# An encoder layer on one core: the merge gates go to the end of the first stage, and an input is exchanged by halves

## The chip, the cores and the metric

The kernel runs on one core of a Trainium2 chip. Its time is the device time of one execution in microseconds, and the figure compared is the median of several runs. The engines are TensorE (PE, with PEld for its weight loads), VectorE (DVE), ScalarE (ACT), GpSimd (POOL) and SyncE (SP). SyncE only issues DMA transfers; all of this kernel's transfers go through its one queue, in order.

## The reference

The layer takes 2048 tokens of 1024 channels in float32. One RMS-normalised input `h` feeds three token mixers, whose outputs are merged by gates that are computed from the same `h`:

```
h = rmsnorm(x, g_mix); z = h @ w_in          # 5648 columns, 3072 of them for the gates
gates = sigmoid(gate_pre)                    # 3 branches x 1024 channels
y = gates0*(h_m @ w_proj_mlstm) + gates1*(h_na @ w_proj_na) + gates2*(h_mem @ w_proj_mem)
x = x + y @ w_out
out = x + square(relu(rmsnorm(x, g_ffn) @ w_up)) @ w_down
```

`h_m` is a bidirectional mLSTM (a recurrence over the tokens in both directions), gated by `o`, another 512 columns of `z`. `h_na` is a neighbourhood attention over a 32 x 64 grid of tokens. `h_mem` is a cross attention into 256 memory tokens.

## The kernel before

Every large product is made of three TensorE matmuls (`mm3`, L228): both factors are split into a high and a low part, and high*high, high*low and low*high are summed in PSUM. A unit of weights is a tile of 128 x 1024 values; `fetch` (L155) loads one with a DMA (`wr`) and has ScalarE and VectorE, for every fourth unit GpSimd, split it (`ws`). `take` hands units out in the order that `plan` (L139) wrote down. TensorE's instructions run in the order in which the program writes them. The order on the other engines, SyncE's queue too, is set when the program is built, by a scheduler that goes by priorities and by its own estimate of when operands are ready.

The tokens are worked on in four blocks of 512. The tile `hT` holds the split, normalised input of one block, transposed, as 8 k tiles of 128 channels; there is one such tile.

Stage 1 (`phase_1`, `block_a`) runs block by block the products with `w_in`: q and k of the attention, q and k of the mLSTM, v, gates (for blocks 2 and 3 alone, `GATES_1`), and o. Gates are 24 groups of 24 matmuls with one weight unit each (`gate`, L596); o is four groups of 24. Each group's result is taken out of PSUM by ScalarE into a tile `ev` (two buffers in stages 1 and 2) and stored. After every second k tile, `tick` (L106) lets side work go one step: the attention's small matmuls and softmax rows (`na_stream`), the cross attention, preparation of the next block's input. Blocks 0 and 1 store their `hT` to DRAM (`SPILL`).

Stage 2 (`phase_2`) runs the mLSTM's recurrence as side work (`ml_stream`, which starts after 20 ticks) beside the gates of blocks 1 and then 0, which need those inputs back (`late_gates`, L603). Gates that are left when the recurrence ends run at the start of stage 3. `ml_consts` and `ml_logsig` set up stage 2: constants, and two `ev` tiles, for the raw row of `g_mlstm` (scaled into `gml` at L710) and for the log of the forget gates. Stage 3 is the merge, the output projection and the MLP.

So `hT` is exchanged twice. The first exchange is at the end of stage 1: each o group of block 3 frees one slice of 128 tokens, and block 1's slice is loaded there (L559 to L567), the last one in eight small transfers. The second is in stage 2, between the gates of block 1 and those of block 0: four transfers of 1 MB, one for every two k tiles, and four ticks without gates (L607 to L611).

`sums_down` (L569) is other work that lies beside the gates. It prepares operands for the last product of stage 3: per call two loads of 512 KB, four VectorE subtractions (L580) and two stores of 512 KB, with low priority. It is called after every third gate, 8 times in block 2 and 8 times in block 3.

Of the kernel before, what the change touches and what calls it, by code (L numbers as in the profile page):

```python
# [12 lines left out]
F32 = mybir.dt.float32  # L13
F32R = mybir.dt.float32r
BF16 = mybir.dt.bfloat16
AF = mybir.ActivationFunctionType
# [8 lines left out]
LOW, LATER, LATER_A, SOON = 100, 60, 60, 40  # L25
TICKS_2, START_2 = 4, 20
PAD = 192
# [9 lines left out]
NB = S // TB  # L37
# [5 lines left out]
GATES_1, GATES_2 = [2, 3], [1, 0]  # L43
# [36 lines left out]
class Body:  # L80
# [58 lines left out]
    def plan(self):  # L139

        u = unit_index()
        self.down = u["down"]
        out = list(u["w_mem_kv"])
        for b in range(NB):
            for n in ("naqk", "qk", "navm", "v"):
                out += u[n]
            if b in GATES_1:
                out += u["gate"]
            out += u["o"]
        for g in GATES_2:  # L150
# [341 lines left out]
    def block_a(self, b):  # L492
# [42 lines left out]
        for t in range(4):  # L535
# [5 lines left out]
            self.store(self.scr["v"][b][t * 128:(t + 1) * 128], s)  # L541
        if b in GATES_1:
            for j in range(24):
                if j == 22 and b + 1 < NB:
                    self.prep_x()
                self.gate(b, j)
                if j % 3 == 2:
                    self.sums_down(8 * GATES_1.index(b) + j // 3)
        w = self.take(4)
        for t in range(4):  # L550
# [7 lines left out]
            self.store(self.scr["og"][b][t * 128:(t + 1) * 128], s)  # L558
            if b == NB - 1:  # L559
                ts = slice(t * 128, (t + 1) * 128)  # L560
                src = self.scr["hT"][GATES_2[0]]
                if t < 3:
                    nc.sync.dma_start(hT[:, :, :, ts].bitcast(F32), src[:, :, :, ts])
                else:
                    for k in range(0, 8, 2):
                        for l in range(2):
                            nc.sync.dma_start(hT[:, l, k:k + 2, ts].bitcast(F32), src[:, l, k:k + 2, ts])  # L567

# [27 lines left out]
    def gate(self, b, j):  # L596
# [4 lines left out]
        self.store(self.scr["gate"][b][j], s)  # L601

    def late_gates(self, more):  # L603

        while self.gq and more():
            b, j = self.gq.pop(0)
            if j == 0 and b != GATES_2[0]:  # L607
                for k in range(0, 8, 2):
                    self.nc.sync.dma_start(self.hT[:, :, k:k + 2].bitcast(F32), self.scr["hT"][b][:, :, k:k + 2])
                for _ in range(TICKS_2):  # L610
                    self.tick()  # L611
            self.gate(b, j)

# [949 lines left out]
```

## Time and profile before

| | us |
|---|---|
| median of 3 runs (lowest, highest) | 3026.33 (3022.54, 3032.49) |
| the profiled execution's own time | 3031.61 |
| its span, first to last instruction | 3029.9 |
| PE busy | 2923.0 (96%) |
| DVE busy | 2079.8 (69%) |
| ACT busy | 1199.8 (40%) |
| POOL busy | 432.5 (14%) |

Times in the rows are counted from the span's start. Stage 1 reaches from 0 to about 990, stage 2 to about 1400. "[9.13 <-X]" behind an instruction says that its engine stood idle for 9.13 us before it and that X ended the wait. A tile's name before the arrow is written, those behind it are read: `mm<-hT,ws` is a gate's matmul, `tr<-ident,nsb` a transpose of softmax rows. Matmuls overlap, so a matmul of 0.39 us starts 0.23 us after the one before it.

### The profile page before, as it was taken

Reading aid. Unit: us, or ns where it says so; the run is one execution under the profiler, and the core shown is the slowest. Engines: PE = TensorE matmul, PEld = TensorE weight load, DVE = VectorE, ACT = ScalarE, POOL = GpSimd, SP = SyncE. Lnnn points to the kernel's source line nnn. Section 1 sums busy time; section 2 is a strip of 40 time slices with the busy share of each in tenths; the row PEclk is TensorE's granted clock in tenths of the full one; section 3 lists DMA queues with packets and bytes.
Section 4 is the critical chain, followed back from the end, with each engine's and each line's share of the span. In section 5 each row is a group of like instructions: output and inputs, shape, how many; then the busy total and the mean of one; then the engine's idle time right before and its main releaser. Section 6 shows DMA issues by size and latency. Waiting matters only on the chain.

```text
span 3029.9 us, 41928 instructions
## 1 busy us (share of the span) xinstructions
PE 2923.0 (96%) x15028; PEld 2381.9 (79%) x15028; DVE 2079.8 (69%) x3386; ACT 1199.8 (40%) x2198; POOL 432.5 (14%) x488
## 2 busy tenths in 40 slices
PE   8899999989999799999999999999999999999999
PEld 7778788768778667677888888888788888888887
DVE  6566776457664765664869888766676888885666
ACT  6454554345543333333234333543322433345331
POOL 5232321123001432341100000000000000000000
PEclk9999999999999999999999999999999999999999
DMA  7676777776789766788734444766774444456555
GB/s 277 195 243 194 218 232 242 241 235 211 208 266 309 218 202 202 238 250 301 248 111 151 153 153 153 271 195 224 254 239 140 128 168 153 153 206 228 193 186 166
DMA packets 341712, 632.97 MB, mean 209 GB/s; under 512 B 29344, under 2 KB 151008, under 8 KB 341504
## 3 DMA queue, kind: packets, MB, share of 16 engines
q1 hardware_dynamic: 341504, 630.30, 64.5%
q8 instruction: 118, 1.93, 0.3%
q14 instruction: 90, 0.74, 0.1%
HBM read 453.63 MB, written 176.55 MB: 208 GB/s over the span
## 4 chain that ended last, share of the span: by engine, by line
PE 65%; DVE 7%; DMA 4%; issue 2%; SPq 1%; ACT 1%; POOL 1%; POOLq 0%; DVEq 0%; ACTq 0%
PE mm L233 20%; PE mm L235 20%; PE mm L234 20%; DMA wr<-in_w_units_dram 1%; DVE ws L178 1%; PE tr L1049 1%; PE pn L863 1%; DVE h L901 1%; DVE dw L580 0%; PE mx L1063 0%; PE mx L1030 0%; DMA nab<-in_rpb_dram 0%; DMA hf<-s_hf 0%; DMA dw<-in_w_units_dram 0%; PE pn L866 0%
## 5 line engine op out<-in xcount | busy, mean ns | idle before, releaser
L233 PE MATMUL mm<-X,ws 128*128 128x512 f32 x1152 | 448.5, 389 | 0.0
L235 PE MATMUL mm<-X,ws 128*128 128x512 f32 x1152 | 448.2, 389 | 0.0
L234 PE MATMUL mm<-X,ws 128*128 128x512 f32 x1152 | 448.1, 389 | 0.0
L233 PE MATMUL mm<-hT,ws 128*128 128x512 f32 x896 | 377.8, 422 | 14.6 <-DMA hT<-s_hT 9.1
L235 PE MATMUL mm<-hT,ws 128*128 128x512 f32 x896 | 354.9, 396 | 0.0
L234 PE MATMUL mm<-hT,ws 128*128 128x512 f32 x896 | 354.3, 395 | 0.0
L234 PE MATMUL mm<-X 128*128 128x512 f32 x896 | 348.8, 389 | 4.0 <-DVE X L1449 4.0
L235 PE MATMUL mm<-X 128*128 128x512 f32 x896 | 348.7, 389 | 0.3 <-DVE X L1449 0.3
L233 PE MATMUL mm<-X 128*128 128x512 f32 x896 | 348.6, 389 | 0.0
L1448 ACT ACTIVATE X<-X 128x1024 fp32r<-128x1024 f32 x176 | 186.6, 1062 | 324.6 <-DMA X<-s_t 136.5
L1449 DVE TENSOR_TENSOR X<-X 128x1024 fp32r<-128x1024 f32 x176 | 214.0, 1223 | 139.9 <-ACT X L1448 138.8
L178 POOL TENSOR_TENSOR ws<-wr,ws 128x1024 fp32r<-128x1024 f32 (+1 forms) x53 | 134.1, 2530 | 1110.5 <-DVE X L1449 623.9
L175 ACT ACTIVATE ws<-wr 128x1024 fp32r<-128x1024 f32 (+1 forms) x212 | 222.9, 1057 | 159.5 <-PE mm L235 85.0
L233 PE MATMUL mm<-ws,hT 128*128 128x512 f32 (+2 forms) x704 | 264.5, 376 | 6.5 <-ACT cz L655 6.1
L178 DVE TENSOR_TENSOR ws<-wr,ws 128x1024 fp32r<-128x1024 f32 (+1 forms) x159 | 206.2, 1301 | 91.7 <-ACT ws L175 91.6
L235 PE MATMUL mm<-ws,hT 128*128 128x512 f32 (+2 forms) x704 | 252.1, 358 | 0.1
L234 PE MATMUL mm<-ws,hT 128*128 128x512 f32 (+2 forms) x704 | 251.8, 358 | 0.1
L235 PEld LDWEIGHTS mm<-X,ws 128*128 128x128 f32 x1152 | 216.2, 188 | 45.1
L234 PEld LDWEIGHTS mm<-X,ws 128*128 128x128 f32 x1152 | 216.3, 188 | 44.8
L233 PEld LDWEIGHTS mm<-X,ws 128*128 128x128 f32 x1152 | 216.2, 188 | 44.5
L203 ACT ACTIVATE ws<-wr 128x512 fp32r<-128x512 f32 x224 | 135.0, 628 | 219.8 <-PE mm L235 139.6
L233 PEld LDWEIGHTS mm<-hT,ws 128*128 128x128 f32 x896 | 170.8, 191 | 58.9 <-issue 18.0
(268 smaller groups left out, 5139.4 us busy)
## 6 DMA issues: line engine op xcount, KB each, us to landing
wr<-in_w_units_dram SPq DMA_DIRECT2D x308, 512.0 KB
s_s<-u SPq DMA_DIRECT2D x32, 1024.0 KB
X<-s_s SPq DMA_DIRECT2D x64, 512.0 KB
X<-s_t SPq DMA_DIRECT2D x64, 512.0 KB
s_g<-ev SPq DMA_DIRECT2D x96, 256.0 KB
ev<-s_g SPq DMA_DIRECT2D x96, 256.0 KB
s_a<-u SPq DMA_DIRECT2D x96, 256.0 KB
X<-s_a SPq DMA_DIRECT2D x48, 512.0 KB
```

What stands on the lines that cost most here:

```text
L175: nc.scalar.activation(w[:, 0], raw, AF.Copy)
L178: eng.tensor_tensor(w[:, 1], raw, w[:, 0].bitcast(F32), ALU.subtract)
L203: nc.scalar.activation(hi, src, AF.Copy)
L233: mm(out, lhs[0], rhs[0], start=first, stop=False)
L234: mm(out, lhs[0], rhs[1], start=False, stop=False)
L235: mm(out, lhs[1], rhs[0], start=False, stop=last)
L863: nc.tensor.matmul(pn[h % 2][:, j], pt[:, h], v1[:, h], start=True, stop=first)
L901: nc.vector.scalar_tensor_tensor(h[:, i], h[:, i], rs[:, i:i + 1], og[:, i * 128:(i + 1) * 128], ALU.mult, ALU.mult)
L1049: nc.tensor.transpose(ptp[0:120, j], sb[:, j * 120:(j + 1) * 120], self.ident)
L1448: nc.scalar.activation(hi, src, AF.Copy)
L1449: nc.vector.tensor_tensor(lo, src, hi.bitcast(F32), ALU.subtract)
```

## The change

Three things change. In block 3 the o groups come before the gates (in `plan` too), and the loads of `hT` among the o groups go. In blocks 2 and 3 `sums_down` is called after every second of the first 16 gates instead of after every third of 24. And around both exchanges the last two gates of the old block and the first two of the new one are worked in pairs (`two_gates`): both gates' k tiles 0 to 3, then both gates' k tiles 4 to 7; after each half of an old block's pair, the two transfers that reload this half of `hT` follow. The four ticks at the second exchange go.

```
-            if b in GATES_1:
-                out += u["gate"]
-            out += u["o"]
+            out += u["gate"] + u["o"] if b == 2 else u["o"] + u["gate"] if b == NB - 1 else u["o"]
...
-        if b in GATES_1:
-            for j in range(24):
-                if j == 22 and b + 1 < NB:
-                    self.prep_x()
-                self.gate(b, j)
-                if j % 3 == 2:
-                    self.sums_down(8 * GATES_1.index(b) + j // 3)
+        if b in GATES_1 and b + 1 < NB:
+            self.gates(b)
...
-            if b == NB - 1:
...
+        if b == NB - 1:
+            self.gates(b)
+
+    def gates(self, b):
+        for j in range(0, 24, 2):
+            if j == 22 and b + 1 < NB:
+                self.prep_x()
+            if j == 22 and b + 1 == NB:
+                self.two_gates(b, j, GATES_2[0])
+            else:
+                self.gate(b, j)
+                self.gate(b, j + 1)
+            if j < 16:
+                self.sums_down(8 * GATES_1.index(b) + j // 2)
...
+    def two_gates(self, b, j, then=None):
+        nc = self.nc
+        w = self.take(2)
+        ps = [self.ps("mm") for _ in w]
+        for k0 in (0, 4):
+            for i, (u, p) in enumerate(zip(w, ps)):
+                for k in range(k0, k0 + 4):
+                    self.mm3(p, (u[:, 0, k], u[:, 1, k]), (self.hT[:, 0, k], self.hT[:, 1, k]), k == 0, k == 7)
+                    if k % 2:
+                        self.tick()
+                if k0:
+                    s = self.ev()
+                    nc.scalar.activation(s, p, AF.Tanh, scale=0.5)
+                    self.store(self.scr["gate"][b][j + i], s)
+            if then is not None:
+                for k in range(k0, k0 + 4, 2):
+                    nc.sync.dma_start(self.hT[:, :, k:k + 2].bitcast(F32), self.scr["hT"][then][:, :, k:k + 2])
...
             b, j = self.gq.pop(0)
-            if j == 0 and b != GATES_2[0]:
-                for k in range(0, 8, 2):
-                    self.nc.sync.dma_start(self.hT[:, :, k:k + 2].bitcast(F32), self.scr["hT"][b][:, :, k:k + 2])
-                for _ in range(TICKS_2):
-                    self.tick()
-            self.gate(b, j)
+            if j == 0 or j == 22 and b != GATES_2[-1]:
+                self.gq.pop(0)
+                self.two_gates(b, j, GATES_2[-1] if j else None)
+            else:
+                self.gate(b, j)
```

## Rows read from the trace of the kernel before

**Rows 1.** The page: the span, and TensorE's busy time, share and instructions.
```profile
span 3029.9 us, 41928 instructions
...
PE 2923.0 (96%) x15028; PEld 2381.9 (79%) x15028; DVE 2079.8 (69%) x3386; ACT 1199.8 (40%) x2198; POOL 432.5 (14%) x488
```
**Rows 2.** Waits of PE, whole span: us in total, times, longest us.
```profile
PE tr L1049 <- DVE nsb L1038: 23.6, 16, 8.9
PE mm L233 <- DMA hT<-s_hT: 9.1, 1, 9.1
...
PE mm L233 <- ACT ev L600: 5.5, 4, 2.1
```
**Rows 3.** Timeline of PE, first exchange: start us, us, instruction.
```profile
989.38 0.39 PE L235 MATMUL mm<-ws,hT 128*128 128x512 f32 x1
998.89 0.77 PE L233 MATMUL mm<-hT,ws 128*128 128x512 f32 x1 [9.13 <-DMA hT<-s_hT]
...
1013.46 0.50 PE L233 MATMUL mm<-hT,ws 128*128 128x512 f32 x1 [2.07 <-ACT ev L600]
```
**Rows 4.** Timeline of SyncE's queue, first exchange.
```profile
989.93 4.85 SPq L100 DMA_DIRECT2D s_t<-dw  x2
...
995.38 4.69 SPq L567 DMA_DIRECT2D hT<-s_hT  x8
```
**Rows 5.** Timeline of DVE, first exchange.
```profile
993.10 1.28 DVE L580 TENSOR_TENSOR dw<-dw,dw 128x512 f32<-128x512 f32 x2
...
998.46 0.10 DVE L252 MEMSET pad<- 128x48 f32 x1 [2.43 <-DMA hT<-s_hT]
...
1010.60 0.43 DVE L710 TENSOR_SCALAR gml<-ev 128x512 f32<-128x512 f32 x1
```
**Rows 6.** Timeline of ACT, first exchange.
```profile
1011.19 0.31 ACT L730 ACTIVATE ev<-ev 128x128 f32<-128x128 f32 x1 [5.50 <-DVE ev L729]
...
1012.81 0.60 ACT L600 ACTIVATE ev<-mm 128x512 f32<-128x512 f32 x1
```
**Rows 7.** The line of o's evictions, block 3: duration, first and last start us.
```profile
L557 ACT ACTIVATE ev<-mm x4: 597/600/600, 973.5 to 989.9; 128x512 f32<-128x512 f32 x4
```
**Rows 8.** Timeline of SyncE's queue, second exchange: its first transfer.
```profile
1215.33 1.12 SPq L609 DMA_DIRECT2D hT<-s_hT  x1
```
**Rows 9.** DMA view of 1215 to 1223 us: GB/s in 40 equal slices.
```profile
GB/s 284 51 10 92 399 356 358 49 13 23 31 225 154 0 143 184 410 348 389 430 389 471 389 451 410 410 307 123 41 0 0 0 0 0 0 0 0 0 0 0
```
**Rows 10.** Timeline of PE, second exchange.
```profile
1223.57 1.12 PE L828 MATMUL mx<-qk 64*128 64x128 f32 x6 [2.33 <-DVE C L878]
```
**Rows 11.** Timeline of PE, block 3: two waits for the attention's work.
```profile
661.56 1.11 PE L1049 MATMUL tr<-ident,nsb 128*120 128x128 f32 x4 [8.92 <-DVE nsb L1038]
...
862.87 0.71 PE L1030 MATMUL mx<-nak,naq 96*128 96x440 f32 x1 [3.99 <-DMA nab<-in_rpb_dram]
```
**Rows 12.** Timeline of DVE ahead of the first of them.
```profile
645.63 0.68 DVE L580 TENSOR_TENSOR dw<-dw,dw 128x512 f32<-128x512 f32 x1
...
648.50 2.88 DVE L580 TENSOR_TENSOR dw<-dw 128x512 f32<-128x512 f32 x1
...
652.45 3.42 DVE L580 TENSOR_TENSOR dw<-dw,dw 128x512 f32<-128x512 f32 x2
```
**Rows 13.** Timeline of POOL at the same time.
```profile
647.69 3.15 POOL L178 TENSOR_TENSOR ws<-wr,ws 128x1024 fp32r<-128x1024 f32 x1 [2.23 <-ACT ws L175]
652.60 2.72 POOL L417 TENSOR_TENSOR xt<-xt,gbc 128x1024 f32<-128x1024 f32 x1 [1.77 <-DVE xt L415]
```
**Rows 14.** The line of gates' evictions, blocks 2 and 3: first and last start us.
```profile
L600 ACT ACTIVATE ev<-mm x24: 576/600/602, 460.2 to 621.1; 128x512 f32<-128x512 f32 x24
...
L600 ACT ACTIVATE ev<-mm x24: 574/600/602, 787.4 to 968.1; 128x512 f32<-128x512 f32 x24
```
**Rows 15.** Stretches: busy us of PE, PEld, DVE, ACT, POOL; PEclk, DMA share, GB/s.
```profile
657.00:667.00 10.00, 5.44 (x15) 4.54 (x16) 6.18 (x16) 3.81 (x9) 0.13 (x1) 0.50 0.90 309
860.00:975.00 115.00, 111.66 (x680) 89.33 (x681) 63.17 (x148) 48.57 (x99) 13.22 (x27) 0.97 0.93 299
```

More of the change, by code (lines that the diff above doesn't have):

```diff
@@ L25 @@
 LOW, LATER, LATER_A, SOON = 100, 60, 60, 40
-TICKS_2, START_2 = 4, 20
+START_2 = 20
 PAD = 192
@@ L558, in block_a @@
             self.store(self.scr["og"][b][t * 128:(t + 1) * 128], s)
-            if b == NB - 1:
[L560 to L564, printed above, removed]
-                    for k in range(0, 8, 2):
-                        for l in range(2):
-                            nc.sync.dma_start(hT[:, l, k:k + 2, ts].bitcast(F32), src[:, l, k:k + 2, ts])
+        if b == NB - 1:
[11 more added lines that the diff above has]
+                self.sums_down(8 * GATES_1.index(b) + j // 2)
     def sums_down(self, q):
@@ L606, in late_gates @@
             b, j = self.gq.pop(0)
-            if j == 0 and b != GATES_2[0]:
-                for k in range(0, 8, 2):
-                    self.nc.sync.dma_start(self.hT[:, :, k:k + 2].bitcast(F32), self.scr["hT"][b][:, :, k:k + 2])
-                for _ in range(TICKS_2):
-                    self.tick()
-            self.gate(b, j)
+            if j == 0 or j == 22 and b != GATES_2[-1]:
[3 more added lines that the diff above has]
+                self.gate(b, j)
     def phase_2(self):
```

## The prediction

> **What bounds the kernel now.** I read the page first: TensorE is busy for 2923.0 of 3029.9 us [rows 1], so this change, which alters no matmul, can only act on the roughly 100 us in which TensorE stands still or runs at the lower of its two clock levels. Next I read TensorE's list of waits [rows 2]. Three of its entries lie where the diff works. The reload of hT costs one wait of 9.1 us. The eviction of gates (L600) costs 5.5 us in four waits. The softmax rows of the neighbourhood attention (nsb), made by VectorE, cost 23.6 us in 16 waits, the longest 8.9 us; the diff doesn't touch their code, but it moves sums_down, which runs on the same VectorE queue. Then I read the timelines of all queues around each of these places, and last the stretches with their DMA share.
>
> **First exchange, before.** The last o group's matmul starts at 989.38 and ends near 989.8; the first late gate starts at 998.89, and the third at 1013.46 after a second wait, of 2.07 us, for the eviction [rows 3]. Without waits two gates take two groups of 24 matmuls. Four o groups, equally long, are evicted from 973.5 to 989.9 [rows 7], so a group takes 16.4 / 3 = 5.47 us and two 10.9 us. From 989.8 to 1013.46 are 23.7 us: 12.8 us are lost, of which 9.1 and 2.1 are the two waits and most of the rest is the matmuls at the lower clock behind the first (0.77 us at 998.89 where 0.39 is usual [rows 3]).
>
> Why is the reload late? SyncE's queue shows it: two stores of sums_down hold it from 989.93 for 4.85 us, and only then, at 995.38, go the eight small transfers of the last token slice [rows 4]. The stores waited for VectorE, whose last two subtractions ran at 993.10 [rows 5].
>
> **First exchange, after.** E is the end of stage 1's last matmul. The last pair of gates is done with k tiles 0 to 3 at E - 5.5 us, and two transfers of 1 MB follow. Nothing of sums_down should be in their way, because its last call now stands after gate 15. The nearest rows are the second exchange's: a transfer issued at 1215.33 [rows 8] shows up as 400 GB/s between about 1218.0 and 1220.6 in slices of 0.2 us [rows 9]. So 1 MB lands some 5.3 us after issue, and a second one 2.6 us later. Landed at E and E + 2.6, they are wanted at E and E + 1.4: 1 to 2 us of waiting. The other half is issued near E, lands by E + 6 to E + 8, and is wanted from about E + 7: 0 to 1 us. So the 9.1 us wait becomes about 1.5 (bounds 0 and 9.1).
>
> But that wait covered another chain. Stage 2's tiles lie where stage 1's were, so its setup begins when stage 1's last stores have landed: VectorE's first instruction of it is the memset at 998.46, E + 8.7. It ends with the scaling of gml at 1010.60 [rows 5]. The first late gate needs the ev tile that gml's raw row holds until then, and it is evicted on ScalarE behind the setup's logarithm, which itself waited 5.50 us for VectorE: at 1012.81 [rows 6], 14.35 us after the setup's start. Nothing in the diff shortens that chain. After the change its start hangs on the store of gate 23, issued about 1 us after E and landed at E + 4 alone, or E + 8 behind the 2 MB of the second half; I take E + 6. So gate 0 is evicted at E + 20.4 and the third gate starts at E + 21, where before it was E + 23.7. TensorE will be through with its two gates by E + 12.5 and will then wait some 8 us for the eviction. Behind waits of that length it runs at the lower level for a while (granted 0.50 in 657 to 667, behind the 8.92 us wait [rows 11, 15]); I charge 2 us. Sum: -2.7 + 2 = about **-1 us**. Bounds: -11 (setup no longer in the way, only 1.5 of 12.8 left) and +3 (setup at E + 8, lower clock for 3 us).
>
> **Second exchange.** Before, the four reloads go out as gate 23 of block 1 frees its k tiles, and four ticks without gates fill the gap. The only stop there is 2.33 us for VectorE's state update [rows 10]. The list of waits has a single one for hT, the first exchange's [rows 2], so there is none here to remove. The four ticks' recurrence work isn't removed either: it goes beside a gate that otherwise stands in stage 3. I take **0**; bounds -4 (that stop and the lower clock behind it go) and +4 (another such stop).
>
> **sums_down, every second gate instead of every third.** One call loads 1 MB, makes four subtractions and stores 1 MB. In block 2 gates are evicted from 460.2 to 621.1, 7.0 us apart; in block 3 7.9 us [rows 14].
> - *End of block 2.* The longest nsb wait, 8.92 us at 661.56 [rows 11], ends on a VectorE queue in which the last call stands just ahead: its four subtractions took 0.68, 2.88 and, for two, 3.42 us [rows 12] where two took 1.28 [rows 5], because GpSimd worked on a weight and on x beside them (647.69 for 3.15 us, 652.60 for 2.72 [rows 13]). They hold VectorE for 7.0 us. Behind the wait TensorE is granted 0.50; 5.44 us of work [rows 15] cost another 2.7. After the change block 2's last call stands eight gates earlier and block 3's first comes only after o and two gates, so this pile should go and leave 1.5 of 11.6 us: -10. Against it I set 3 us for collisions of the same kind elsewhere in block 2, now that eight calls share 16 gates (the other nsb waits, 23.6 - 8.9 = 14.7 us over 15 stops, average 1 us). Together **-7**; bounds -11.6 and +4 (the pile stays and new ones are added).
> - The Trainium skill, "SBUF — State Buffer", section "Who interferes with whom", says that a VectorE instruction with two SBUF inputs and a GpSimd instruction that reads SBUF exclude each other for a whole instruction. By that rule 4 of the 7 us come from GpSimd and would return wherever a call meets GpSimd's share of weights; by the trace, which shows both instructions side by side, the meeting is as long as that rule says. It would leave -10 here and put up to 4 us on each new meeting.
> - *Block 3.* DMA engines are 0.93 busy at 299 GB/s over 860 to 975 [rows 15], so about 320 GB/s is all that this mix gets. A call's 2 MB came every 24 us and now comes every 16: +42 GB/s, 341 asked of 320, over some 110 us 2.3 MB or 7 us of backlog. Its loads can be late without harm, but the attention's bias rows stand in the same queue, and one such wait is there already (3.99 us at 862.87 [rows 11], about 7 with the lower clock behind it). o ahead of the gates gives the queue a rest first. I take **+2**; bounds -7 (that wait goes) and +14 (two more).
> - The Trainium skill, "DMA: Bandwidth & Descriptors", section "Where 436 GB/s comes from", gives about 358 GB/s between HBM and SBUF. By that figure 341 would fit and this term be 0 or below; by the row, 299 at a share of 0.93, it does not fit.
>
> **Sum.** -1 + 0 - 7 + 2 = -6 us on the profiled execution of 3031.6 us: 3025.6. That execution is 5.3 us above the median of the runs, 3026.3, so I forecast a median of 3020. Differences under 0.3% (9 us) can't be told from none here.
>
> **Rivals.**
> 1. *The setup does not bind.* The chain of setup starts earlier or frees its ev tile earlier, and both waits of the first exchange go: -11 instead of -1, -16 in all, 3010. For it: gml's scaling is one short instruction that could run before the constants. Against it: it ran 12 us after the setup's first instruction [rows 5], and nothing in the diff moves it up. Chance 0.2.
> 2. *The pile at the end of block 2 only moves.* Block 3's first call fills the same hole in the queues; its term is 0 to +2, and the sum +2: 3028. For it: a call's loads wait only for a free tile and a free place in SyncE's queue, not for their gates. Chance 0.25.
> 3. *Slower.* In block 3 the denser sums_down makes the bias rows late: SyncE's queue is in order, a store of sums_down waits on VectorE, which waits on a load in full queues, and the attention's loads stand behind. Each such stop costs 4 + 3 us. From three new stops on (+21) it outweighs the 8 us of the other terms: +13, 3039. Against it: 860 to 975 was almost as full [rows 15], and the list names that one stop. Chance 0.13.
> 4. My forecast, 3020: 0.42.
>
> **How the numbers follow.** Rival 1 lies beyond 9 us of gain, and about 0.4 of the forecast's own spread (sd some 7 us) does: 0.2 + 0.16 = 0.36 faster. Rival 3 with a little of rival 2 gives 0.13 slower; the rest, 0.51, is within 0.3%. The range runs from 3007 (rival 1 with a little more) to 3034 (between rivals 2 and 3).
>
> **What would show it.** In the profile after: the wait of TensorE on hT at the first exchange under 3 us; in its place a wait of 5 to 10 us on the eviction at L600 before the third late gate; no hT wait at the second exchange; no nsb wait above 4 us near the start of block 3; DMA share near 1.0 for the first 16 gates of block 3 and much lower in the last eight. The forecast is wrong if the third late gate starts without that wait, if a long nsb wait remains between blocks 2 and 3, or if waits on bias rows in block 3 sum to more than 10 us.

## The result, and the profile after

| | before | after |
|---|---|---|
| median of 6 runs each, side by side (lowest, highest), us | 3028.02 (3022.54, 3036.76) | 3043.26 (3037.77, 3049.91) |
| the profiled execution's own time, us | 3031.61 | 3043.82 |
| its span, us | 3029.9 | 3041.4 |

The ratio is 1.0048 [1.0033, 1.0063]: the change makes the kernel slower. I had forecast 3020 with a range up to 3034, and given "slower" a chance of 0.13. The medians differ by 15 us; the two profiled executions differ by 11.5 us in their spans, and the points below account for these 11.5.

The page after, its span and TensorE's row, against [rows 1]:

```profile
span 3041.4 us, 41940 instructions
...
PE 2925.9 (96%) x15028; PEld 2382.7 (78%) x15028; DVE 2077.5 (68%) x3386; ACT 1199.8 (39%) x2198; POOL 432.9 (14%) x488
```

TensorE does the same work in 2.9 us more of busy time (2923.0 before); the rest of the 11.5 us is standing still. Where it stands is read by lining up the two traces: as the order of TensorE's products is the program's, the start of the n-th matmul in the one trace can be subtracted from that in the other. Every stretch in which the difference grows has lost time. The points are the start of block 2's gates, the start of block 3, the end of block 3, the first gates of stage 2, and the end. All later tables of this kind are made the same way, against the profiled execution before.

| matmul no. (its time before, us) | 2600 (459) | 4600 (795) | 5700 (967) | 6000 (1051) | 15000 (3017) |
|---|---|---|---|---|---|
| after, us later than before | -1.4 | +1.7 | +19.4 | +10.5 | +11.5 |

So on these two executions block 2 and its end cost 3.1 us, block 3 costs 17.7, the first exchange gives back 8.9, and all the rest of the kernel is within 2.4. The list of TensorE's waits after, whole span, names the places (us in total, times, longest), against [rows 2]:

```profile
PE tr L1067 <- DVE nsb L1056: 27.2, 17, 8.4
...
PE mx L1048 <- DMA nab<-in_rpb_dram: 6.8, 1, 6.8
PE mx L1048 <- issue: 6.5, 1, 6.5
```

The wait of 9.1 us on hT has left the head of the list. Two stops on the attention's scores (L1048) are new, and the longest wait on softmax rows (nsb) is 8.4 us where it was 8.9. In TensorE's timeline after (start us, us, instruction) these three stand here, in the order of time, the first against the 8.92 us stop of [rows 11]:

```profile
656.40 1.08 PE L1067 MATMUL tr<-ident,nsb 128*120 128x128 f32 x4 [8.44 <-DVE nsb L1056]
...
903.81 0.61 PE L1048 MATMUL mx<-nak,naq 96*128 96x320 f32 x1 [6.54 <-issue]
...
941.05 0.61 PE L1048 MATMUL mx<-nak,naq 96*128 96x320 f32 x1 [6.78 <-DMA nab<-in_rpb_dram]
```

**Block 3's stops.** L1048 multiplies a new head group's q by its k (naq, nak). It doesn't read the bias rows nab: the releaser is inferred, and nab stands for the queue behind q and k. SyncE's queue after, with some lines left out, shows why they are late (start us, us, issue):

```profile
884.02 1.55 SPq L576 DMA_DIRECT2D dw<-in_w_units_dram  x2
885.61 0.51 SPq L1015 DMA_DIRECT2D naq<-s_qs  x1
886.17 0.45 SPq L1016 DMA_DIRECT2D nak<-s_ks  x1
...
894.97 2.12 SPq L100 DMA_DIRECT2D s_t<-dw  x2
897.14 0.46 SPq L1015 DMA_DIRECT2D naq<-s_qs  x1
897.65 0.82 SPq L1016 DMA_DIRECT2D nak<-s_ks  x1
...
899.53 1.85 SPq L1032 DMA_DIRECT2D nab<-in_rpb_dram  x4
```

The first third of q and k goes out at 885.61. Then the queue issues nothing from 886.62 to 894.97, 8.35 us, since next in it stand the stores of sums_down, whose subtractions VectorE runs at 893.29 and after. The other two thirds go out from 897.14, and the scores start at 903.81. The second stop is the same picture: nak at 924.20, the stores at 932.43, the next naq at 934.19. The Trainium skill, "DMA: Bandwidth & Descriptors", section "Anatomy of one DMA — SWDGE (gpsimd) path", says that DMA engines don't wait on semaphores: the wait is taken by the sequencer that issues, before it dispatches. The trace agrees for SyncE's queue: for 8.35 us the other two thirds of q and k were not issued, though the first third had already gone into the same two tiles.

I had put such a backlog down to full DMA engines. Windows after over 40 us around each stop, over the stretch of [rows 15], and over the two parts of the first hold (window, its length, busy time (instructions) of PE, PEld, DVE, ACT, POOL, then PEclk, DMA share, GB/s):

```profile
870.00:910.00 40.00, 32.36 (x204) 25.73 (x203) 22.15 (x50) 15.09 (x32) 3.39 (x9) 0.91 0.88 289
910.00:950.00 40.00, 33.22 (x205) 26.25 (x207) 21.86 (x55) 15.94 (x34) 3.52 (x10) 0.91 0.86 287
860.00:975.00 115.00, 99.73 (x617) 79.44 (x616) 66.58 (x156) 45.74 (x97) 10.30 (x28) 0.94 0.85 280
...
886.00:892.00 6.00, 6.00 (x58) 4.65 (x57) 3.92 (x7) 4.43 (x8) 2.46 (x2) 1.00 1.04 363
892.00:896.00 4.00, 4.00 (x24) 3.36 (x22) 4.00 (x11) 1.27 (x4) 0.20 (x2) 1.00 0.19 46
```

and, from the kernel before, over the same two stretches of 40 us:

```profile
870.00:910.00 40.00, 39.87 (x277) 31.76 (x276) 25.70 (x63) 19.98 (x41) 3.91 (x12) 1.00 0.88 283
910.00:950.00 40.00, 39.66 (x253) 31.54 (x252) 23.63 (x62) 19.33 (x44) 6.77 (x13) 1.00 0.99 306
```

Over 860 to 975 they were 0.93 busy before and are 0.85 busy after. During the hold they are full as long as the call's loads move, and from 892 to 896 they have next to nothing to do. Part of the fall can be the stops themselves, in which TensorE uses up no weights. A share alone doesn't tell where a stop will be: the kernel before has 0.88 over 870 to 910 and 0.99 after that, without a stop in either.

**End of block 2.** VectorE's timeline after, from the softmax row's sum to its scaling, against [rows 12]:

```profile
645.55 0.08 DVE L1051 DVE_READ_ACCUMULATOR2_ANT sm<- 128x1 f32 x1
645.83 2.90 DVE L413 TENSOR_TENSOR xt<-xt,gmix 128x1024 f32<-128x1024 f32 x1 [0.20 <-DMA xt<-in_xT_dram]
648.66 4.49 DVE L176 TENSOR_TENSOR ws<-wr,ws 128x1024 fp32r<-128x1024 f32 x2
653.07 0.15 DVE L1055 RECIPROCAL sm<-sm 128x1 f32<-128x1 f32 x1
653.14 2.75 DVE L433 TENSOR_TENSOR hT<-xt,hT 128x512 fp32r<-128x512 f32 x1
655.82 0.44 DVE L1056 TENSOR_SCALAR nsb<-nsb,sm 128x440 f32<-128x440 f32 x1
```

The subtractions of sums_down are gone from here, as I had said. In their place stand a product on block 3's x tile, two weight splits and a split into hT: 10.1 us of others' work around the two short instructions (0.15 and 0.44 us) that TensorE waits for.

**First exchange.** TensorE's timeline after, the first four gates of stage 2 and the last matmul before them, against [rows 3]:

```profile
1008.74 0.39 PE L233 MATMUL mm<-hT,ws 128*128 128x512 f32 x1
...
1012.38 0.50 PE L231 MATMUL mm<-hT,ws 128*128 128x512 f32 x1 [0.85 <-DMA hT<-s_hT]
1017.38 0.50 PE L231 MATMUL mm<-hT,ws 128*128 128x512 f32 x1 [0.64 <-DMA hT<-s_hT]
1019.84 0.50 PE L231 MATMUL mm<-hT,ws 128*128 128x512 f32 x1 [0.80 <-DMA hT<-s_hT]
1027.22 0.69 PE L231 MATMUL mm<-hT,ws 128*128 128x512 f32 x1 [3.00 <-ACT ev L616]
```

With E = 1009.1 the third gate starts at E + 18.1, where it was E + 23.7: 5.6 of the 8.9 us are there by then. Stage 2's setup starts at E + 4.9 (VectorE's memset at 1014.01) and gate 0 is evicted 12.56 us after that. ScalarE's timeline after shows the eviction ahead of the logarithm's table load, where [rows 6] has it behind the logarithm:

```profile
1026.57 0.60 ACT L616 ACTIVATE ev<-mm 128x512 f32<-128x512 f32 x1 [5.40 <-DVE gml L728]
...
1028.32 1.28 ACT L748 ACT_TABLE_LOAD   x1
```

### The profile page after: what moved, and what is told of

Same layout as the page of the kernel before. It is cut to its first block, busy times and chain, and to the rows that moved or that the text cites. A ratio compares the mean times of both kernels' runs of the same rounds, so it can differ in the third digit from the quotient of the medians.

```text
span 3041.4 us, 41940 instructions
## 1 busy us (share of the span) xinstructions
PE 2925.9 (96%) x15028; PEld 2382.7 (78%) x15028; DVE 2077.5 (68%) x3386; ACT 1199.8 (39%) x2198; POOL 432.9 (14%) x488
## 4 chain that ended last, share of the span: by engine, by line
PE 69%; DVE 5%; DMA 4%; issue 2%; ACT 1%; SPq 1%; POOL 1%; DVEq 0%; ACTq 0%; POOLq 0%
PE mm L231 22%; PE mm L233 21%; PE mm L232 21%; PE tr L1067 1%; DMA wr<-in_w_units_dram 1%; DVE ws L176 1%; PE pn L881 1%; DMA dw<-in_w_units_dram 1%; DMA X<-s_hm 1%; PE mx L1081 1%; PE pn L884 1%; PE mx L1048 0%; DMA s_g<-ev 0%; PE mm L1344 0%; ACT ws L173 0%
## 5 line engine op out<-in xcount | busy, mean ns | idle before, releaser
L1467 DVE TENSOR_TENSOR X<-X 128x1024 fp32r<-128x1024 f32 x176 | 214.5, 1223 | 140.0 <-ACT X L1466 139.2
```

The source lines that it names most:

```text
L1467: nc.vector.tensor_tensor(lo, src, hi.bitcast(F32), ALU.subtract)
```

## The experiments

All ratios are against the kernel before, timed on the same chip. "A" is the changed kernel, "B" the kernel before. The first seven ask about the exchange and block 3.

**e4_second_exchange_alone.** B with the second exchange of the change alone.

```
-            self.gate(b, j)
+            if (b, j) in ((GATES_2[0], 22), (GATES_2[1], 0)):
+                self.gq.pop(0); self.two_gates(b, j, GATES_2[-1] if j else None)
+            else: self.gate(b, j)
```

> The kernel before with the second exchange alone done by halves and without its four ticks. My prediction's step: nothing to gain, since no wait for hT was there; 0 us, within 4 us either way, 0.9985 to 1.0015. Rival: the four ticks without gates were what the recurrence's waits behind them came from; then 5 us or more of faster.

Measured: 3029.45 us, 0.9999 [0.9987, 1.001]. The second exchange is worth nothing, in either direction.

**e2_dense_in_block3_only.** B with sums_down after every second gate in block 3; order of o, exchanges and block 2 as before.

```
-                if j % 3 == 2:
-                    self.sums_down(8 * GATES_1.index(b) + j // 3)
+                if b + 1 < NB and j % 3 == 2: self.sums_down(j // 3)
+                if b + 1 == NB and j % 2 and j < 16: self.sums_down(8 + j // 2)
```

> The kernel before with one thing changed: block 3 calls sums_down after every second of its first 16 gates. Theory A: stops of 4 to 7 us on bias rows appear in block 3 and the time rises by 8 to 18 us, to 1.002 to 1.006; the wait for hT at the first exchange gets shorter than 9.1 us since the last call lies eight gates earlier, which takes 3 to 9 us off again. Rival B (the order of o and gates): no new stops, the time falls by the 3 to 9 us.

**e1_block3_every_third.** A with block 3's calls after every third gate again.

```
                 self.gate(b, j)
+                if b + 1 == NB and j % 3 == 2: self.sums_down(8 + j // 3)
                 self.gate(b, j + 1)
-            if j < 16:
+            if b + 1 == NB and (j + 1) % 3 == 2: self.sums_down(8 + (j + 1) // 3)
+            if b + 1 < NB and j < 16:
                 self.sums_down(8 * GATES_1.index(b) + j // 2)
```

> The changed kernel, but block 3 calls sums_down after every third of its 24 gates, as before; block 2 keeps the new spacing, o stays ahead of the gates, the halves stay. Theory A: the two stops of the changed kernel at 903.8 and 941.1 us (6.5 and 6.8 us, and the lower clock behind them) come from the denser calls in block 3, whose stores stand in SyncE's queue ahead of the attention's q, k and bias loads and wait for VectorE. Then these stops shrink to one at most and the time falls by 10 to 18 us against the changed kernel, to 0.994 to 1.001 of the kernel before. Rival B: o ahead of the gates has shifted the attention's loads against the gates' work. Then the stops stay and the time is 1.003 to 1.006.

Measured: e2 3049.44 us, 1.006 [1.0045, 1.0076]; e1 3049.13 us, 1.0059 [1.0044, 1.0074]. The waits of TensorE between 500 and 1080, in e2:

```profile
PE mx L1032 <- DMA nab<-in_rpb_dram: 14.4, 2, 7.2
PE mx L1032 <- issue: 7.0, 1, 7.0
...
PE mm L233 <- DMA hT<-s_hT: 4.2, 1, 4.2
```

and in e1:

```profile
PE mm L231 <- ACT ev L620: 16.3, 1, 16.3
PE mx L1052 <- DMA nab<-in_rpb_dram: 7.8, 2, 7.4
```

Density alone makes stops in block 3: e2 has three of 7 us, where B has one of 3.99 [rows 11]. e1, with the old spacing and the new order, keeps one of 7.4, so its block 3 still loses 5.2 us (table below) and its time misses what was expected. Density also shortens the exchange: in e2, which keeps the old exchange, the wait on hT falls from 9.1 to 4.2 us, for sums_down is done earlier. Its third gate starts here:

```profile
1027.39 0.50 PE L233 MATMUL mm<-hT,ws 128*128 128x512 f32 x1 [0.95 <-ACT ev L602]
```

e2's last matmul of stage 1 ends at 1009.2, so this is E + 18.2, and A has E + 18.1. Up to the third gate, then, the early end of sums_down gives all that the change gives at the first exchange; that the exchange by halves adds something is not shown. (The rest of A's gain comes behind that gate, where B's gates wait 0.75 and 2.00 us for evictions and A's don't; e2 has a stop of 4.29 us there.) e1 shows the other side. Its last call's loads go out at 1010.05, past the end of the stage, its stores at 1018.75, and since stage 2's tiles lie where these stood, its setup begins with them landed:

```profile
1018.75 1.71 SPq L100 DMA_DIRECT2D s_t<-dw  x2
```

```profile
1023.37 0.10 DVE L250 MEMSET pad<- 128x48 f32 x1 [3.32 <-DMA s_t<-dw]
```

The third gate then waits 16.3 us for its ev tile. So neither spacing is good with o ahead of the gates: dense, the calls stop block 3; sparse, they hold up stage 2.

**e6_block3_calls_only_store.** A; block 3's calls store a constant tile and leave out their loads and subtractions, 1 MB of 2 MB each.

```
-        r = [self.t("dw", [128, 1024], 2) for _ in range(2)]
-        for half in range(2):
+        r = [self.t("dw", [128, 1024], 2) if q < 8 else self.gbc for _ in range(2)]
+        for half in range(2 if q < 8 else 0):
...
-        for out, x, y in (...):
+        for out, x, y in (...) if q < 8 else ():
```

> The changed kernel, but in block 3 sums_down loads and subtracts nothing and stores a constant tile: 1 MB a call instead of 2, no wait. What it leaves out are block 3's loads and subtractions. Theory A2: with half of the bytes ahead of them and no wait, the stops shrink to under 2.5 us each and the time falls by 12 to 20 us against the changed kernel. Rival (where the attention stands against the gates, whatever sums_down does): the stops stay within 2 us of 6.5 and 6.8.

**e3_stores_that_do_not_wait.** A; block 3's stores read a constant tile (the sums_down operand is left out of the result), loads and subtractions stay.

```
-            self.store(self.scr["t"][q // 2][:, half, :, q % 2], r[half].rearrange(...))
+            self.store(self.scr["t"][q // 2][:, half, :, q % 2], (r[half] if q < 8 else self.gbc).rearrange(...))
```

> The changed kernel, but the stores of sums_down in block 3 take their data from a constant tile, so that they carry the same bytes and wait for no subtraction; what they store is not the operand. Loads and subtractions stay. Theory A (the stores' wait holds SyncE's queue): the two stops go, the time falls by 10 to 18 us, to 0.994 to 1.001 of before. Rival C (too many bytes for the DMA engines, as my prediction argued): the bytes are the same, so the stops stay, and the time is 1.003 to 1.006.

**e5_qk_a_unit_earlier.** A; the next head group's q and k are asked for one unit of the attention earlier, ahead of the loads that held them.

```
                 last = self.na_unit(*todo.pop(0), last)
+                if last["half"] and todo:
+                    self.qk_next = self.na_load_qk(*todo[0][:2])
```

> The changed kernel, but the attention's q and k of the next group are asked for one unit (some 15 us) earlier, so that only its bias and value loads still stand behind sums_down's transfers. Theory A2: the stops at 903.8 and 941.1 us come because a new group's six q and k loads, its bias and its values stand in SyncE's queue behind a call's 2 MB, whether the queue is held by the store's wait or full of bytes. Then both stops shrink from 6.5 and 6.8 to under 2.5 us, block 3's loss against the kernel before (18 us) falls to 5 or less, and the time is 0.996 to 1.0005 of before. Rival: it is the bias rows' own buffers (they wait for the rows in use) that make the loads late; then the stops stay above 4 us and the time is 1.003 or more.

Measured: e6 3023.25 us, 0.9978 [0.9966, 0.9989]; e3 3042.52, 1.0039 [1.0023, 1.0055]; e5 3038.27, 1.0022 [1.0009, 1.0035]. By the table, in us against B, with block 3 the difference of its two columns:

| | 2600 | 4600 | 5700 | 6000 | 15000 | block 3 |
|---|---|---|---|---|---|---|
| A, after | -1.4 | +1.7 | +19.4 | +10.5 | +11.5 | +17.7 |
| e2, dense only | -1.7 | -5.2 | +19.4 | +15.2 | +17.3 | +24.6 |
| e1, every third | -1.6 | +2.7 | +7.9 | +13.2 | +17.2 | +5.2 |
| e6, no loads | -5.6 | 0.0 | -2.8 | -9.9 | -9.0 | -2.8 |
| e3, stores don't wait | -5.1 | +3.2 | +16.7 | +8.4 | +10.1 | +13.5 |
| e5, q and k earlier | +8.1 | +5.4 | +11.4 | +2.5 | +9.0 | +6.0 |

Without the loads and the wait that hangs on them block 3 loses nothing (e6; with them go half of the calls' bytes, so it doesn't part wait from bytes). Taking the stores' wait alone away brings back only some 4 of 17.7 us, and that is hardly a difference: kernels with A's calls in block 3 (A, e7, e12, e13, e16, e18) lose between 15.2 and 20.4 us there. e3's queue, some lines left out, shows what remains:

```profile
870.94 10.17 SPq L1032 DMA_DIRECT2D nab<-in_rpb_dram  x4
...
884.89 2.05 SPq L576 DMA_DIRECT2D dw<-in_w_units_dram  x2
886.99 1.03 SPq L100 DMA_DIRECT2D s_t<-gbc  x2
888.30 0.33 SPq L1015 DMA_DIRECT2D naq<-s_qs  x1
...
893.81 0.30 SPq L1016 DMA_DIRECT2D nak<-s_ks  x1
```

The queue is held all the same, by bias rows that wait for one of four tiles, and what it then lets out at once, sums_down's loads and stores first, stands ahead of q and k in the DMA engines: six issues of q and k take from 888.30 to 894.11, and the window is full:

```profile
870.00:905.00 35.00, 29.18 (x193) 23.36 (x192) 19.99 (x48) 14.18 (x29) 3.31 (x8) 0.96 0.99 301
```

So my theory that the stores' wait makes the stops holds in part: in A it is what holds the queue, but without it a burst does nearly the same (stops of 5.83 and 4.93 us at the same two places). e3 and e6 differ by the calls' loads and subtractions, and by 16 us in block 3. What takes the stops away with all of the calls' work still there is q and k ahead of it: in e5 the list of waits between 500 and 1080 has none on the scores. Stops of the gates on their evictions appear instead:

```profile
PE mm L232 <- ACT ev L600: 13.8, 4, 6.9
```

B has 5.5 us there [rows 2], over the whole span. Besides, the profiled execution has lost 8.1 us before block 2's gates. By the ratios, 1.0048 and 1.0022, some 8 of 15 us are won, less than I had expected. The long stop at the end of block 2 is gone in e5 as well: no wait on softmax rows between 500 and 1080 is above 2.7 us.

**e8_before_with_qk_earlier.** The same edit on B, whose one stop of 3.99 us it should take away.

> The kernel before with the attention's q and k asked for one unit earlier and nothing else. Theory A2: its one stop on bias rows (4.0 us at 862.9, 3 more of lower clock) goes, -3 to -7 us, 0.9975 to 0.999 of before. Rival: the stop is the bias rows' own buffers and stays, 1.000.

Measured: 3041.79, 1.0041 [1.0025, 1.0056], a miss. The stop goes, but gates wait six times on evictions, 10.6 us, and block 3 wins nothing (+1.0); 4.4 us are lost ahead of block 2's gates and 5.7 behind matmul 6000. The edit pays only where the stops are.

**e9_twelve_and_four.** A with 12 of the 16 calls in block 2's gates and 4 in block 3's.

```
-            if j < 16:
-                self.sums_down(8 * GATES_1.index(b) + j // 2)
+            if b + 1 < NB: self.sums_down(j // 2)
+            elif j in (0, 4, 8, 12): self.sums_down(12 + j // 4)
```

> The changed kernel, but twelve of the sixteen sums_down calls lie in block 2 (one after every second gate) and four in block 3 (after gates 1, 5, 9 and 13). Theory A3: block 3's loss (17.7 us against the kernel before between the 4600th and the 5700th matmul) is set by how many bytes of sums_down meet the attention's loads there; with half of the calls, spread twice as wide, the loss is under 4 us, while the first exchange stays as cheap as in the changed kernel, because the last call lies early: 12 to 18 us less than the changed kernel, 0.997 to 1.0005 of before. Rival: block 2 then has the stops instead, 1.002 or more.

Measured: 3043.28, 1.0037 [1.0023, 1.005], a miss. Block 3 loses 6.3 us instead of 17.7, but block 2 now loses 12.7, with stops of its own at 632, 663 and 685. The stops go where the calls go.

**e12_gml_row_of_its_own.** A with gml's raw row in a tile of its own, so that no gate waits for the setup to give an ev tile back.

```
-        raw = self.ev()
+        raw = t("gml_raw", [128, 512])
```

> The changed kernel with a tile of its own for gml's raw row, which took the ev tile that the first late gate's eviction waits for. My prediction's claim: stage 2's setup holds the third late gate through this tile. Then the wait of 3.0 us for the eviction at 1027.2 us goes and the time falls by 2 to 5 us against the changed kernel. Rival: the eviction waits behind the log's instructions on ScalarE's queue; then the wait stays or grows.

Measured: 3040.12, 1.0031 [1.002, 1.0043]. The third gate and the fourth start here:

```profile
1022.23 0.39 PE L231 MATMUL mm<-hT,ws 128*128 128x512 f32 x1
...
1029.38 0.50 PE L231 MATMUL mm<-hT,ws 128*128 128x512 f32 x1 [1.55 <-ACT ev L616]
```

The third gate's wait is gone: with E = 1007.8 it starts at E + 14.4 instead of E + 18.1. So the tile that gml's raw row holds was the whole of that wait, as I had claimed. The rival's wait comes one gate later: the fourth waits 1.55 us for the second gate's eviction, which stands behind the logarithm and its table loads on ScalarE. By matmul 6000 the exchange gives back 10.4 us instead of 8.9.

The others ask about the 8.44 us stop at the end of block 2.

**e7_x_rows_on_vectore.** A; the product of x with its row factor goes from GpSimd to VectorE, so that GpSimd has no part of the x tiles any more.

```
-            nc.gpsimd.tensor_tensor(xt, xt, rb.unsqueeze(1).to_broadcast([128, 8, 128]), ALU.mult)
+            nc.vector.tensor_tensor(xt, xt, rb.unsqueeze(1).to_broadcast([128, 8, 128]), ALU.mult)
```

> The changed kernel, but the product of x with its row factors runs on VectorE instead of GpSimd (12 instructions). It asks what the stop of 8.4 us at 656.4 us is, which my prediction put down to sums_down and which the changed kernel has with no subtraction near it. Theory D: VectorE's instructions with two inputs stand still while GpSimd reads (2.90, 4.49 for two, 2.75 us there); then without GpSimd's products the stop shrinks to 2 to 5 us although VectorE has 1.2 us more for each. Rival: VectorE is simply given too much in front of the softmax there; then the stop stays or grows.

Measured: 3034.1, 1.0013 [1.0003, 1.0022]. The stop is still 8.04 us, a miss for theory D. The time fell elsewhere: at matmul 2600 it is 13.5 us ahead of B (A 1.4), won in blocks 0 and 1. So the edit was put on two other kernels.

**e11_before_x_on_vectore** and **e10_twelve_four_x_on_vectore.** The same edit on B, and on e9.

> The kernel before with x's row factors on VectorE alone. If the 12 us of blocks 0 and 1 come from GpSimd's share and not from the change, it is 0.995 to 0.997 of before.

> The twelve-and-four kernel with x's row factors on VectorE as in the run before. That run gained 12 us before the 2000th matmul, in blocks 0 and 1. If the two are independent, the sum is 0.993 to 0.9965 of before, faster than both kernels; if the gain in blocks 0 and 1 was a chance of the order of the queues, it is that of the twelve-and-four kernel.

Measured: e11 3017.52, 0.996 [0.9948, 0.9973], faster than both kernels; e10 3029.17, 0.9997 [0.9986, 1.0008]. The gain of e11 is there by matmul 2600 (-12.1) and stays (-12.7 at the end). e10 misses its range because e9 had missed its own; against e9 (1.0037) it gains the same 12 us.

**e15_qk_earlier_x_on_vectore.** A with the edits of e5 and e7.

> The changed kernel with the attention's q and k asked for one unit earlier and the row factors of x on VectorE. Theory (the two work at different places: block 3's stops, and blocks 0 and 1): the gains of 5 and 9 us add up, about 3029, 0.9995 of the kernel before. Rival (both put work on the same queue order and the gains don't add, as with q and k earlier on the kernel before): 3033 or more.

Measured: 3028.69, 0.9989 [0.9979, 0.9999]. The two gains add up, as forecast: block 3 loses 5.2 us, and the change is paid for, no more.

**e13_x_tile_twelve_gates_earlier**, **e14_before_x_on_vectore_tile_earlier.** A and e11, with the call for block 3's first x tile at gate 10 instead of 22.

```
-            if j == 22 and b + 1 < NB:
+            if j == 10 and b + 1 < NB:
```

> The changed kernel, with the first x tile of block 3 asked for and prepared at gate 10 of block 2 instead of gate 22. Theory (the stop at the boundary comes from two x tiles prepared at once, 1.23 and 2.90 us on VectorE ahead of the softmax row's scaling): the 8.44 us stop falls below 4 us, TensorE's 4600th matmul comes about 6 us earlier against the changed kernel, the time is about 3037 (8.44 and 2 us of lower clock, less 4 that other work still takes). Rival (weight splits and hT splits alone fill VectorE's queue there): a stop of 7 us or more stays within 20 us of the boundary, the time is 3043. Second rival (the place moves): a stop of 5 us or more appears in gates 10 to 16 of block 2 instead, where sums_down's subtractions run.

> The kernel before with the row factors of x on VectorE (3017.5 in an earlier run, with a stop of 7.67 us left at the boundary of blocks 2 and 3) and the first x tile of block 3 prepared at gate 10 of block 2. Theory: the 7.67 us stop falls below 4 us and the time is about 3010, 0.993 of the kernel before. Rival (sums_down's subtractions and weight splits make the stop here): it stays at 6 us or more and the time is 3017.

**e16_second_x_tile_in_the_gates**, **e17_before_x_on_vectore_second_tile.** The same two kernels, with the calls for the first two x tiles at gates 10 and 16 and none at the first o group.

> The changed kernel, with the first two x tiles of block 3 prepared at gates 10 and 16 of block 2, instead of at gate 22 and at the first o group. Theory (two x tiles prepared side by side, on VectorE and GpSimd, hold the softmax row's scaling): only one is left at the boundary, the stop of 8.44 us falls below 5 us, and the time is 4 to 6 us less, about 3038. Rival (the two weight splits, 4.49 us, and the hT split, 2.75 us, suffice): a stop of 6.5 us or more stays there, and the time is 3042 or more.

> The kernel before with the row factors of x on VectorE, and the first two x tiles of block 3 prepared at gates 10 and 16 of block 2. Theory: of the four x products that stand on VectorE near its 7.8 us stop (1.2 us each) two go, the stop falls to about 5 us, and the time to about 3014, 0.995 of the kernel before. Rival (sums_down's subtractions and the weight splits, 0.69 + 2.36 + 2.89 + 1.28 + 1.21 us there, make it): it stays at 7 us or more and the time at 3018.

Measured: e13 3047.05, 1.0048 [1.0029, 1.0067]; e14 3021.53, 0.9961 [0.9946, 0.9975]; e16 3048.25, 1.0056 [1.0036, 1.0076]; e17 3019.05, 0.9958 [0.9939, 0.9976]. The stops stay at 7.92, 7.82, 7.33 and 7.18 us. These four tell nothing on the cause, because the edits moved nothing: the first tile was loaded at 508.61 in A already, long before its call's place, and the second and third still come together in e16 (641.70 and 642.65). The order on the queues is the scheduler's, not the program text's.

Another edit did move the tiles, without being made for it. In A the two products with g_mix start at 643.88 and 645.83, in e5 at these times:

```profile
653.07 1.23 DVE L414 TENSOR_TENSOR xt<-xt,gmix 128x1024 f32<-128x1024 f32 x1 [2.82 <-DMA xt<-in_xT_dram]
...
654.87 2.53 DVE L1062 TENSOR_SCALAR nsb<-nsb,sm 128x440 f32<-128x440 f32 x1
...
658.76 1.23 DVE L414 TENSOR_TENSOR xt<-xt,gmix 128x1024 f32<-128x1024 f32 x1
```

A row is scaled between the two, and the longest stop is 2.7 us, though both products and four subtractions of sums_down run on VectorE between 643 and 660. In e15 the two tiles are 5.6 us apart, and no stop on softmax rows between 500 and 1080 is longer than 2.3 us. So these products do little harm where a row's scaling does not stand behind all of them. But e5 also moves the attention's loads, and no weight split falls into that stretch, so this is no clean test of the two tiles.

**e18_no_products_on_block_3_x.** A without the two products on block 3's x tiles; g_mix and the row factor are left out there.

```
+            if b < NB - 1:
                 nc.vector.tensor_tensor(xt, xt, self.gmix..., ALU.mult)
                 nc.gpsimd.tensor_tensor(xt, xt, rb..., ALU.mult)
```

> The changed kernel; block 3's x tiles are split without the two products (g_mix and row factor left out), so VectorE is rid of 1.23 + 2.90 us and GpSimd of 2.41 + 3.21 us at the boundary of blocks 2 and 3. Theory (the x preparation makes the 8.44 us stop, by its own time and by having GpSimd beside VectorE): the stop falls below 4 us. Rival (the weight splits, 4.49 us, and the hT split, 2.75 us, suffice): a stop of 5.5 us or more stays, as long as the first of them still stands between the softmax row's sum and its scaling. Time: 3038 by the theory, 3042 by the rival.

Measured: one execution, 3031.43 us, beside 3036.03 of B. Its waits, whole span:

```profile
PE mx L1049 <- DMA nab<-in_rpb_dram: 18.3, 2, 10.9
PE tr L1068 <- DVE nsb L1057: 16.5, 15, 1.8
```

No wait on softmax rows above 1.8 us is left, although VectorE makes the same splits there:

```profile
644.29 0.45 DVE L1057 TENSOR_SCALAR nsb<-nsb,sm 128x440 f32<-128x440 f32 x1
645.05 1.23 DVE L176 TENSOR_TENSOR ws<-wr,ws 128x1024 fp32r<-128x1024 f32 x1 [0.30 <-ACT ws L173]
...
646.79 1.22 DVE L176 TENSOR_TENSOR ws<-wr,ws 128x1024 fp32r<-128x1024 f32 x1
```

Between matmuls 2600 and 4600 it wins 7.1 us against B, where A loses 3.1. So without the products on block 3's x A's stop goes. The rival isn't refuted as it was put: the splits come behind the scaling here, not ahead of it, so what they would do in its way isn't shown. Block 3 loses 18.9 us as in A, with stops of 10.9 and 7.4 us: the two places are separate. By what path the products do it, by their own 4.1 us on VectorE or by pushing the splits behind them, this run doesn't tell. e7, with both products on VectorE, has the stop too.

## Why the prediction was wrong

In the order of its steps, predicted against measured on the profiled executions: first exchange -1 and -8.9, second exchange 0 and 0, end of block 2 -7 and about +3, block 3 +2 and +17.7. The +3 is the least sure of them, as kernels with the same block 2 (A, e1, e3, e6, e12) lose between 0.2 and 8.3 us there. The remaining +1.0 - 1.4 are smaller than what two executions of a kernel differ by. The sum was to be -6 and is +11.5.

*Block 3 is the step that failed most*, by 15.7 us. The step is the term of +2: it let the backlog of sums_down fall where nothing waits ("its loads can be late without harm"), and put only the bias rows at risk. The runs show it falling on q and k, for which TensorE does wait. Two thirds of a new group's q and k stood behind a call in the one queue that issues in order: in A behind stores that wait for subtractions, which wait for loads; in e3, where no store waits, behind the call's loads and stores themselves. e2 and e6 show the dense calls as the cause, and e5, which keeps every call and asks for q and k earlier, shows the place of q and k in the queue as what makes most of the harm. How much of the 17.7 us is the hold and how much the bytes is not parted: e3 takes only the hold away and wins about 4, not clear of noise.

The sum of bytes itself was off as well. I took 320 GB/s for what the mix gets, by stretching 299 at a share of 0.93; at a share of 0.99 it got 301 (e3) and 306 (B, 910 to 950). By 301, 341 GB/s over 110 us would have left some 15 us of backlog and not 7 (an estimate from these rows).

Rival 3 says nearly this, with 7 us a stop, three stops and 3039 us in all; there were two, of 6.5 and 6.8 us of waiting, and 17.7 us lost around them. It named the bias rows, and q and k are the tiles for which TensorE waits. I gave it 0.13 because "860 to 975 was almost as full", an argument on bandwidth against a rival on order.

The Trainium skill's figure of about 358 GB/s ("DMA: Bandwidth & Descriptors", section "Where 436 GB/s comes from"), by which the 341 would have fitted, was not reached by the mix: 301 GB/s stand at a share of 0.99 in e3. It is no upper bound either: the slices of 0.2 us in [rows 9] show 348 to 471 GB/s, 410 in the mean, while one transfer of 1 MB moves. For the mix [rows 15] was the better guide, and what stands behind the calls mattered more than the limit.

*End of block 2.* I read the four subtractions ahead of the scaling [rows 12] and took the stop for theirs. They are gone and the stop is 8.44 us: the x tiles' products, and the splits behind them, now stand between the row's sum and its scaling (10.1 us in all), and without the products the stop goes (e18). Rival 2 has this outcome (a term of 0 to +2), with another filler than it named: block 3's first call has nothing to do with it. The Trainium skill, "SBUF — State Buffer", section "Who interferes with whom", has the rule that a VectorE instruction with two SBUF inputs and a GpSimd instruction that reads SBUF exclude each other. The rows still agree with it in size: a product on x takes 2.90 us beside GpSimd's 2.41, and 1.23 alone. But freeing GpSimd of x took only 0.4 us from the stop (e7): VectorE has two products of 1.2 us more there, and one weight split still takes 3.38 us, beside a split on GpSimd of 2.34.

*First exchange.* The two forms of loss came as I had said, less hT (2.3 us in three waits, 1.5 predicted) and a wait on the eviction in its place. The mechanism that I named holds: the third gate waits for the ev tile that gml's raw row holds (e12). Only its size was off. That wait was 3.00 us, not 8: the setup began at E + 4.9 instead of E + 6; gate 0 was evicted 12.56 us after that instead of 14.35, because its eviction ran ahead of the logarithm and its table load, behind which it had stood before; and the first two gates, with their waits, were done at E + 15.1 instead of E + 12.5. What I credited to the halves, though, e2 has without them. Rival 1's -11 is nearer than my -1 by the number alone: its condition, that the setup does not bind, is not met.

*Second exchange.* Right: no wait on hT there before or after, and e4 measures 0.9999.

Of what was to show it: hT under 3 us, yes; a wait of 5 to 10 us before the third gate, no; no hT wait at the second exchange, yes; no nsb wait above 4 us near block 3's start, no; a DMA share near 1.0 in the first 16 gates of block 3 and much lower in the last eight, no (0.88 and 0.86 around the stops, 0.86 over 955 to 1005). Two of the three conditions under which the forecast was to be wrong hold: the long nsb wait, and stops at block 3's loads of 13.3 us in all, though on q and k.

The fastest version found is B with x's row factors on VectorE (e11, 0.996; e14 and e17 are the same within noise); A gains as much from the same edit and then stands at 1.0013. A version of the change that beats B was not found; e15 comes to 0.9989 [0.9979, 0.9999], behind e11.

## What to carry to other kernels

When one queue issues all transfers, don't ask only whether the DMA engines have room for work that is packed closer: list what in the queue waits for an engine or moves many bytes, and which load that TensorE needs soon stands behind it. When a stop ends on a filled queue, the instruction just ahead is not yet its cause: leave each candidate out once, and see what closes up. And an edit that moves a call in the program need not move the transfer, where a scheduler sets the order; look for the issue in the trace before the time is read.

## What was not expected of the hardware

Between 860 and 975 the DMA engines were less busy after the change than before (0.85 against 0.93), while the one queue stood still for 8.35 and 7.6 us; at the end of the first of these holds they had next to nothing to do (a share of 0.19 from 892 to 896). And GpSimd's product on x is dearer to the kernel than VectorE's: with it on VectorE, blocks 0 and 1 end 12 us earlier though VectorE has more to do (e11; 11 to 14 us against B in e7, e10, e14 and e17 too). That the two engines hold each other up there is likely from the rows above, but it was not tested in blocks 0 and 1.
